# A hybrid layer's delta-rule scan: V and output of every other pair of heads in the other half of the partitions, and the streams' steps in a written order

## The chip, the cores and the metric

The kernel runs on one core of one Trainium2 chip. A core has five engines with queues of their own: TensorE for matmuls (PE; PEld is its weight load), VectorE (DVE), ScalarE (ACT), GpSimd (POOL) and SyncE (SP), which here issues most DMAs. The metric is the device time of one execution in microseconds; less is better.

## The reference

One decoder layer on 512 tokens of width 1024, all in float32. A normed input goes through one projection `w_in`; half of it feeds block-sparse attention with 8 heads, the other half a gated DeltaNet with 8 heads of width 64. Their outputs go side by side through `w_out`, then follow a residual, a norm and a squared-ReLU MLP of width 4096. The part that the change is about is the DeltaNet's scan over 8 chunks of 64 tokens:

```python
m = jnp.where(strict, jnp.einsum('bhnid,bhnjd->bhnij', k_beta, kc) * decay, 0.0)
a_mat = m + jnp.eye(C, dtype=jnp.float32)
rhs = jnp.concatenate([vc * bc[..., None], k_beta * jnp.exp(g_cum)[..., None]], axis=-1)
uw = lax.linalg.triangular_solve(a_mat, rhs, left_side=True, lower=True, unit_diagonal=True)
u, w = uw[..., :dh], uw[..., dh:]
attn_intra = jnp.einsum('bhnid,bhnjd->bhnij', qc, kc) * decay
...
def step(state, xs):
    u_c, w_c, q_c, k_c, a_c, gl = xs
    v_new = u_c - jnp.einsum('bhck,bhkv->bhcv', w_c, state)
    o = jnp.einsum('bhck,bhkv->bhcv', q_c, state) + jnp.einsum('bhcs,bhsv->bhcv', a_c, v_new)
    state = state * gl[..., None, None] + jnp.einsum('bhck,bhcv->bhkv', k_c, v_new)
    return state, o
```

## The kernel before

The large matmuls keep float32 accuracy by three products of a high and a low part (`mm3`: high by high, high by low, low by high); each operand is split by a cast on ACT (`w_hi`, `wo_h`, `mg_h`) and a subtraction on DVE or POOL (`w_lo`, `wo_l`, `mg_l`). The program has three stretches. From the start to about 250 us, PE makes the projections' matmuls (`ps_mm<-hT_h,w_hi` and the like), and attention, the chunks' matrices, their inverses and the scan are woven in between. The output projection (`output`, L953) follows up to about 294 us, and the MLP fills the rest.

What is woven are Python generators, called streams: `chunks` makes each pair's matrices (its `turned`, L533, copies gates into the tile `R` on ACT, PE transposes `R`, and ACT and DVE make `RC`, which PE multiplies by `picks`), `inverse` the triangular inverse, `scores` and `values` the attention, `scan` (L776) the delta rule, `finish_o` (L905) its norm, gate and transposes into `mg_h` and `mg_l`; `projections` (L279) is the filler. Each `yield` gives a stream's turn back. The class `Weave` (L49) keeps a modelled PE time, `now`, and always resumes the stream of the best `RANK` whose waiting time, given by the tables `WAIT` (L20) and `SINGLE` (L22), has passed. So PE's order is fixed by the program. On DVE, ACT and POOL a scheduler places the instructions, and a stream's `LEAD` says how far ahead of the others it may place them.

`scan` holds eight heads as four pairs. For chunk n of tokens (tile t, half c), a PSUM bank `B[n]` of 128 partitions gathers three products: the inverse times V (`ps_g<-vB,inv`, made one step ahead by `ahead`), the state `S` times `LWQ` (the operands for V and for the output side by side), and `AT` times V (`ps_g<-vn,AT`). V stands in partitions `cs` of the bank, the output in the other half `oc`; `rows_c` gives both. After `S`·`LWQ`, ACT copies V into `vn` (L870). Then PE makes the state's update (`ps_g<-vn,kdec`) and `AT`·V, with the next chunk's `inv`·`vB` in between:

```python
for h in range(8):
    if sp is not None:
        mm(sp[head(h), h // 2], kdec[cs, t, hs], V[cs, hs], start=True, stop=True)
        if h % 2:
            next(other)()
for h in range(8):
    mm(B[n][oc, h // 2, head(h)], AT[cs, h, t], V[cs, hs], start=n == h == 0, stop=True, skip_group_check=True)
    if h % 2 == 0:
        next(other, lambda: 0)()
```

An output at `head(h)` of the partitions alternates with h between the halves of PE's columns; one at `cs` or `oc` is in one half for the whole step. A small zero matmul (`z`, L855) opens the output's half of the bank. DVE then adds the update into the next state (L893), ACT copies the output to `ot` (L896).

`weights_out` (L935) loads and splits `w_out` in 16 pieces through two `wo_raw` buffers that the projections' loads use as well; SP issues them, ACT casts, DVE subtracts. `weights_up` (L1042) loads the first eight pieces of `w_up`, the last two (k=6, 7) through `w_raw`; `up0` (L1059) multiplies by them. In `normed` (L1010), SP writes a residual tile to `d_x`, and `output` loads the input tile `xs`. At the start, DVE zeroes rows of the two `RC` tiles (L530) ahead of `one`, which FILL=7 warm-up matmuls read in `head` (L217).

Of the kernel before, what the change touches and what calls it, by code (L numbers as in the profile page):

```python
# [35 lines left out]
class Delays(dict):  # L36


    def __init__(self, kinds, single):
        super().__init__(kinds)  # L40
        self.single = single
        self.count = {}

    def __getitem__(self, kind):
        n = self.count[kind] = self.count.get(kind, -1) + 1
        return self.single.get((kind, n), super().__getitem__(kind))


class Weave:  # L49

    def __init__(self, tc):
        self.tc = tc
        self.now = 0.0
        self.marks = {}
        self.live = []

    def spawn(self, rank, stream, lead=0):  # L60
        self.live.append([rank, self.now, stream, lead])
        self.live.sort(key=lambda s: s[0])

    def mark(self, name, wait=0.0):
        self.marks[name] = self.now + wait

    def start(self, s):
        return self.marks.get(s[1], math.inf) if isinstance(s[1], str) else s[1]

    def run(self, until=None):  # L70
        while self.live and not (until and until <= self.marks.keys()):
            s = next((s for s in self.live if self.start(s) <= self.now), None)
            if s is None:
                s = min(self.live, key=self.start)
                assert self.start(s) < math.inf, [s[1] for s in self.live]
                self.now = self.start(s)
            try:
                if s[3]:
                    with self.tc.high_priority(s[3]):
                        w = next(s[2])  # L80
                else:
                    w = next(s[2])
                s[1] = w if isinstance(w, str) else self.now + w
            except StopIteration:
                self.live.remove(s)


def layer(ctx, tc, nc, x, x_t, x_t0, w_first, w_in, w_v, w_ab, w_out, w_up, w_down, conv_w, a_log, dt_bias, gdn_norm_w, rel_bias,
# [9 lines left out]
    def mm(o, l, r, **kw):  # L98
        nc.tensor.matmul(o, l, r, **kw)  # L99
# [1456 lines left out]
```

## Time and profile before

| | |
|---|---|
| runs, median (lowest to highest) | 619.85 us (619.47 to 620.92), 3 runs |
| the profiled execution | 620.34 us; span 618.6 us |
| PE clock granted | 0.998 |
| PE busy 0 to 20 us | 20.00 |
| PE busy 20 to 165 us | 143.33 of 145 |
| PE busy 165 to 250 us (the scan) | 84.34 of 85 |
| PE busy 250 to 300 us | 50.00 |
| PE busy 300 to 618.6 us | 312.50 of 318.6 |

The time of a run is the span and 1.74 us around it. A busy PE need not be PE at its pace: records of matmuls overlap, and where they start further apart than usual, the record is longer, not the idle time. So time is to be read from starts, not from busy shares.

### The profile page before, as it was taken

Reading aid. Unit: us, or ns where it says so; the run is one execution under the profiler, and the core shown is the slowest. Engines: PE = TensorE matmul, PEld = TensorE weight load, DVE = VectorE, ACT = ScalarE, POOL = GpSimd, SP = SyncE. Lnnn points to the kernel's source line nnn. Section 1 sums busy time; section 2 is a strip of 40 time slices with the busy share of each in tenths; the row PEclk is TensorE's granted clock in tenths of the full one; section 3 lists DMA queues with packets and bytes.
Section 4 is the critical chain, followed back from the end, with each engine's and each line's share of the span. In section 5 each row is a group of like instructions: output and inputs, shape, how many; then the busy total and the mean of one; then the engine's idle time right before and its main releaser. Section 6 shows DMA issues by size and latency. Waiting matters only on the chain.

```text
span 618.6 us, 11048 instructions
## 1 busy us (share of the span) xinstructions
PE 607.9 (98%) x4295; PEld 521.9 (84%) x4295; DVE 474.4 (77%) x685; ACT 365.3 (59%) x625; POOL 139.1 (22%) x177
## 2 busy tenths in 40 slices
PE   8999999999999999999999999999999999999996
PEld 7777787878778877788999999999998888888884
DVE  7578873899734576766699878787788888888776
ACT  6479763453686376454338656656665656565663
POOL 0556746100322111025131121123111420000000
PEclk9999999999999999999999999999999999999999
DMA  9232334322721113933669999998999999967503
GB/s 317 84 109 72 95 79 102 105 84 85 173 81 58 52 36 103 315 128 117 242 217 255 225 267 310 263 239 220 237 322 311 304 293 286 310 217 288 183 0 137
DMA packets 61156, 113.22 MB, mean 183 GB/s; under 512 B 15784, under 2 KB 35368, under 8 KB 60720
## 3 DMA queue, kind: packets, MB, share of 16 engines
q1 hardware_dynamic: 43120, 82.89, 39.3%
q0 software_dynamic: 17696, 29.36, 22.8%
q8 instruction: 34, 0.56, 0.4%
q10 hardware_dynamic: 288, 0.26, 0.1%
q14 instruction: 18, 0.15, 0.1%
HBM read 106.71 MB, written 35.15 MB: 229 GB/s over the span
## 4 chain that ended last, share of the span: by engine, by line
PE 81%; issue 10%; DVE 3%; DMA 3%; ACT 2%; SPq 0%; POOLq 0%; DVEq 0%
PE ps_mm L99 40%; PE ps_g L99 22%; PE ps_a L99 16%; PE ps_a L103 2%; DMA wo_raw<-in_w_out 1%; DMA xy<-d_x 1%; PE ps_g L103 1%; DMA E<-d_e 1%; DVE wo_l L145 1%; ACT wo_h L144 0%; DVE L L694 0%; ACT L L696 0%; DVE conv L383 0%; DMA d_e<-L 0%; DVE S L893 0%
## 5 line engine op out<-in xcount | busy, mean ns | idle before, releaser
L132 ACT CAST wdh<-wd 128x1024 fp32r<-128x1024 f32 x53 | 55.9, 1054 | 51.3 <-PE ps_mm L99 22.6
L132 ACT CAST u_h<-w 128x1024 fp32r<-128x1024 f32 x49 | 50.9, 1045 | 52.5 <-DVE w L1166 15.6
L133 DVE TENSOR_TENSOR wdl<-wd,wdh 128x1024 fp32r<-128x1024 f32 x53 | 64.9, 1224 | 21.6 <-ACT wdh L132 21.5
L133 DVE TENSOR_TENSOR u_l<-w,u_h 128x1024 fp32r<-128x1024 f32 x49 | 59.9, 1224 | 23.9 <-ACT u_h L132 23.9
L99 PE MATMUL ps_mm<-hT_h,w_hi 128*128 128x512 f32 x168 | 70.2, 418 | 0.0
L99 PE MATMUL ps_mm<-hT_l,w_hi 128*128 128x512 f32 x168 | 66.0, 393 | 0.0
L99 PE MATMUL ps_mm<-hT_h,w_lo 128*128 128x512 f32 x168 | 65.8, 392 | 0.0
L1199 POOL DMA_DIRECT2D d_T<-in_w_down x32 | 33.0, 1043 | 145.6 <-DMA d_T<-in_w_down 90.7
L156 ACT CAST w_hi<-w_raw 128x512 fp32r<-128x512 f32 x50 | 31.0, 620 | 39.2 <-PE ps_g L99 15.4
L99 PE MATMUL ps_mm<-wdh,u_h 128*128 128x512 f32 x116 | 45.2, 390 | 0.0
L99 PE MATMUL ps_mm<-wdl,u_h 128*128 128x512 f32 x116 | 45.1, 389 | 0.0
L99 PE MATMUL ps_mm<-wdh,u_l 128*128 128x512 f32 x116 | 45.1, 389 | 0.0
L99 PEld LDWEIGHTS ps_mm<-hT_h,w_hi 128*128 128x128 f32 x168 | 31.7, 189 | 8.8 <-issue 2.6
L99 PEld LDWEIGHTS ps_mm<-hT_h,w_lo 128*128 128x128 f32 x168 | 31.5, 188 | 7.1
L99 PEld LDWEIGHTS ps_mm<-hT_l,w_hi 128*128 128x128 f32 x168 | 31.8, 189 | 5.2
L133 DVE TENSOR_TENSOR u_l<-f,u_h 128x1024 fp32r<-128x1024 f32 x28 | 34.1, 1218 | 0.0
L157 POOL TENSOR_TENSOR w_lo<-w_raw,w_hi 128x512 fp32r<-128x512 f32 x22 | 28.8, 1308 | 22.2 <-ACT w_hi L156 18.4
L99 PE MATMUL ps_g<-wdh,u_h 128*128 128x512 f32 x80 | 31.1, 389 | 0.0
L99 PE MATMUL ps_g<-wdl,u_h 128*128 128x512 f32 x80 | 31.1, 389 | 0.0
L99 PE MATMUL ps_g<-wdh,u_l 128*128 128x512 f32 x80 | 31.1, 389 | 0.0
L132 ACT CAST u_h<-f 128x1024 fp32r<-128x1024 f32 x28 | 29.3, 1046 | 0.0
L99 PEld LDWEIGHTS ps_mm<-wdh,u_h 128*128 128x128 f32 x116 | 21.8, 188 | 4.8 <-ACT c_u L1441 0.3
(486 smaller groups left out, 1841.4 us busy)
## 6 DMA issues: line engine op xcount, KB each, us to landing
d_T<-in_w_down POOLq DMA_DIRECT2D x48, 512.0 KB, 11.8
wd<-d_T SPq DMA_DIRECT2D x32, 512.0 KB, 6.3
w<-in_w_up SPq DMA_DIRECT2D x28, 512.0 KB, 8.1
wd<-in_w_down SPq DMA_DIRECT2D x24, 512.0 KB, 8.1
w_raw<-in_w_in SPq DMA_DIRECT2D x40, 256.0 KB, 2.6
wo_raw<-in_w_out SPq DMA_DIRECT2D x16, 256.0 KB, 3.5
d_T<-d_T POOLq DMA_DIRECT2D x8, 512.0 KB, 10.4
ww<-in_w_first SPq DMA_DIRECT2D x8, 256.0 KB, 5.4
```

Of the source, the lines that this page charges most:

```text
L99: nc.tensor.matmul(o, l, r, **kw)
L103: nc.tensor.transpose(o, i, ident[:k, :k])
L132: nc.scalar.copy(hi, src)
L133: tt(lo, src, f32(hi), op=OP.subtract)
L145: (sub or tt)(lo, raw, f32(hi), op=OP.subtract)
L156: nc.scalar.copy(hi, raw)
L157: (sub or tt)(lo, raw, f32(hi), op=OP.subtract)
L1199: nc.gpsimd.dma_start(d_T[t][k], block(b, second)[k], accum_op=OP.add, max_dma_last_dim=1024)
```

## The change

In `scan`, V and the output of pairs 1 and 3 (heads 2, 3, 6, 7) change places: `half(c ^ h // 2 % 2)` puts V of odd pairs in the other half of the partitions of `B[n]`. The order `TURNS` of the heads alternates between even and odd pairs, in `inv`·`vB` and in `AT`·V. The zero matmul is gone (the first two `inv`·`vB` of a bank open it). ACT copies V and the output in two instructions of half the width each; the tile `vn` holds V by parity of the pair. `w_of` and `q_of` swap the places of the two operands in `LWQ` for odd pairs; the negation into `LWQ` and, for q1 and q3, the last operation of `conv_silu` become two of half the size.

`Weave` loses its modelled time. A list `STEPS` names the streams in the order in which they are resumed; a name that isn't ready yet is passed over and stays in the list. The tables `WAIT`, `SINGLE`, `RANK` and `START` go. `LEAD` changes for six kinds, and `ORDER` swaps the projections v0 and v2. The two `RC` tiles are zeroed by POOL. Behind about 300 us the order is the same.

```diff
-RANK = {'chunks': 1, 'inverse': 4, 'scan': 2, 'scores': 4, 'values': 4, 'finish_o': 4, 'take': 3}
-LEAD = {'chunks': 300, 'inverse': 50, 'scan': 50, 'scores': 300, 'values': 50, 'finish_o': 200, 'take': 50, 'take_a': 300, 'scalars': 0}
+STEPS = "constants_in0 chunks1 constants_in0 bias0*3 chunks0 chunks2 chunks3 scalars0*2 ev0 ev1 ...
+LEAD = {'chunks': 100, 'inverse': 50, 'scan': 100, 'scores': 100, 'values': 300, 'finish_o': 200, 'take': 50, 'take_a': 100, 'scalars': 50}
+TURNS = 0, 2, 1, 3, 4, 6, 5, 7
...
-ORDER = "k0 q0 x0 y0 k1 q2 q1 k2 k3 z0 q3 x1 w0 v1 v3 v0 v2 y1 x2 y2 x3 y3 z2 z1 z3"
+ORDER = "k0 q0 x0 y0 k1 q2 q1 k2 k3 z0 q3 x1 w0 v1 v3 v2 v0 y1 x2 y2 x3 y3 z2 z1 z3"
...
-            s = next((s for s in self.live if self.start(s) <= self.now), None)
...
+            name = self.left.pop(next(i for i, name in enumerate(self.left) if self.ready(name)))
+            s = self.live[name]
...
         for t in RCs:
+            nc.gpsimd.memset(f32(t[32:64]), 0.0)
...
-    for t in RCs:
-        nc.vector.memset(f32(t[32:64]), 0.0)
...
-    w_of = lambda p: LWQ[p // 2][:, p % 2, :, 0:4:3]
-    q_of = lambda p: LWQ[p // 2][:, p % 2, :, 1:3]
+    w_of = lambda p: LWQ[p // 2][:, p % 2, :, 1:3] if p % 2 else LWQ[p // 2][:, p % 2, :, 0:4:3]
+    q_of = lambda p: LWQ[p // 2][:, p % 2, :, 0:4:3] if p % 2 else LWQ[p // 2][:, p % 2, :, 1:3]
...
-        stt(dst, f(th), 1.0, f(c), op0=OP.add, op1=OP.mult)
+        for n in ((slice(None), slice(None), 0), (slice(None), slice(None), 1)) if apart else (slice(None),):
+            stt(dst[n], f(th)[n], 1.0, f(c)[n], op0=OP.add, op1=OP.mult)
...
-            for h in range(8):
-                yield lambda h=h: mm(B[n][cs, h // 2, head(h)], UT[cs, h, t], vB[cs, t, 64 * h:64 * h + 64], start=h == 0, stop=False, skip_group_check=True)
-            if n:
-                z = SS[0][cs, 0, 64 - 64 * c:128 - 64 * c]
-                yield lambda: mm(B[n][oc, 0, :64], z, z, start=True, stop=False, skip_group_check=True)
+            for h in TURNS:
+                yield lambda h=h: mm(B[n][half(c ^ h // 2 % 2), h // 2, half(h % 2)], UT[half(c), h, t], vB[half(c), t, 64 * h:64 * h + 64], start=h in (0, 2), stop=False, skip_group_check=True)
...
-                V = sc.tile([128, 512], FT, name="vn", bufs=1)
+                V = sc.tile([128, 2, 2, 128], FT, name="vn", bufs=1)
+                v_of = lambda h: V[cs, h // 2 % 2, h // 4, half(h % 2)]
...
-            nc.scalar.copy(V[cs], B[n][cs].rearrange("p a b -> p (a b)"))
+            for s in range(2):
+                nc.scalar.copy(V[cs, s], of(B[n], s)[half(c ^ s)])
...
-            for h in range(8):
-                hs = slice(64 * h, 64 * h + 64)
-                mm(B[n][oc, h // 2, head(h)], AT[cs, h, t], V[cs, hs], start=n == h == 0, stop=True, skip_group_check=True)
-                if h % 2 == 0:
+            for i, h in enumerate(TURNS):
+                mm(B[n][half(1 - c ^ h // 2 % 2), h // 2, half(h % 2)], AT[cs, h, t], v_of(h), start=False, stop=True, skip_group_check=True)
+                if i % 2 == 1:
                     next(other, lambda: 0)()
...
-            nc.scalar.copy(o[cs], B[n][oc].rearrange("p a b -> p (a b)"))
+            for s in range(2):
+                nc.scalar.copy(of(wide(o), s)[cs], of(B[n], s)[half(1 - c ^ s)])
```

Three places show what the order makes of it. The first is the end of the scan's first step on PE (line, operation, output<-operands, size; line numbers differ between the two programs). Before, with `S` as the zero matmul and the projection's matmul behind it:

```order
L99 MATMUL ps_g<-vn,AT 64x64
L99 MATMUL ps_g<-vB,inv 64x64
L99 MATMUL ps_g<-vn,AT 64x64 x2
L99 MATMUL ps_g<-vB,inv 64x64
L99 MATMUL ps_g<-vn,AT 64x64 x2
L99 MATMUL ps_g<-vB,inv 64x64
L99 MATMUL ps_g<-vn,AT 64x64 x2
L99 MATMUL ps_g<-vB,inv 64x64
L99 MATMUL ps_g<-vn,AT 64x64
L99 MATMUL ps_g<-S_2333 64x64
L99 MATMUL ps_mm<-hT_h_83,w_hi 128x512
```

After:

```order
L82 MATMUL ps_g<-vn,AT 64x64 x2
L82 MATMUL ps_g<-vB,inv 64x64
L82 MATMUL ps_g<-vn,AT 64x64 x2
L82 MATMUL ps_g<-vB,inv 64x64
L82 MATMUL ps_g<-vn,AT 64x64 x2
L82 MATMUL ps_g<-vB,inv 64x64
L82 MATMUL ps_g<-vn,AT 64x64 x2
L82 MATMUL ps_g<-vB,inv 64x64
L82 MATMUL ps_mm<-hT_h_82,w_hi 128x512
```

The `AT` matmuls come by twos from different halves, and the zero matmul is gone. Ahead of this step's `kdec` part stood six matmuls of the projection, and there are fifteen now. For the chunks 1 to 7, the other streams' matmuls and transposes between `S`·`LWQ` and what follows of the scan number 8, 8, 3, 6, 11, 13, 6 before and 6, 11, 6, 6, 9, 16, 15 after; those between the step before and `S`·`LWQ` 6, 7, 24, 12, 3, 3, 6 and 6, 6, 15, 3, 20, 6, 9.

The second is PE between the last transposes of q's squares (`sqt`) and the second transposes of `R`. Before:

```order
L99 MATMUL ps_mm<-hT_h_82,w_lo 128x512
L99 MATMUL ps_mm<-hT_h_82,w_hi 128x512
L99 MATMUL ps_mm<-hT_l_84,w_hi 128x512
L99 MATMUL ps_mm<-hT_h_82,w_lo 128x512
L103 MATMUL ps_g<-ident,R 128x128 x4
L99 MATMUL ps_g<-RC_119,picks 128x512
L99 MATMUL ps_a<-RC_119,picks 128x256 x2
L99 MATMUL ps_g<-RC_119,picks 128x512
L99 MATMUL ps_mm<-hT_h_83,w_hi 128x512
```

After:

```order
L82 MATMUL ps_mm<-hT_h_83,w_lo 128x512
L82 MATMUL ps_mm<-hT_h_83,w_hi 128x512
L82 MATMUL ps_mm<-hT_l_85,w_hi 128x512
L82 MATMUL ps_mm<-hT_h_83,w_lo 128x512
L82 MATMUL ps_g<-RC_119,picks 128x512
L82 MATMUL ps_a<-RC_119,picks 128x256 x2
L82 MATMUL ps_g<-RC_119,picks 128x512
L85 MATMUL ps_g<-ident,R 128x128 x4
L82 MATMUL ps_mm<-hT_h_83,w_hi 128x512
```

The matmuls on `RC` now come ahead of the transposes of `R`; and between the first transposes of `R` (further up) and these stand 24 matmuls of a projection instead of 15.

The third is DVE ahead of the first `mg_l`, which the output projection reads. Before (`wo_l` is a piece of `w_out`, `om` and `zs` the gate of the scan's output, `ot` its norm):

```order
L145 TENSOR_TENSOR wo_l<-wo_raw,wo_h 128x512 x2
L453 SCALAR_TENSOR_TENSOR zs<-t_2899,zs 128x512
L914 TENSOR_TENSOR ot<-ot,oss 128x512
L145 TENSOR_TENSOR wo_l<-wo_raw,wo_h 128x512 x2
L450 SCALAR_TENSOR_TENSOR zs<-ps_mm,rstd_b 128x512
L453 SCALAR_TENSOR_TENSOR zs<-t_2951,zs 128x512
L923 SCALAR_TENSOR_TENSOR om<-ps_g,nw,zs 128x512
L145 TENSOR_TENSOR wo_l<-wo_raw,wo_h 128x512 x2
L133 TENSOR_TENSOR mg_l<-om,mg_h 128x4x128
```

After:

```order
L126 TENSOR_TENSOR wo_l<-wo_raw,wo_h 128x512 x2
L883 TENSOR_REDUCE oss<-osq 128x8
L126 TENSOR_TENSOR wo_l<-wo_raw,wo_h 128x512 x2
L433 SCALAR_TENSOR_TENSOR zs<-ps_mm,rstd_b 128x512
L887 TENSOR_TENSOR ot<-ot,oss 128x512
L436 SCALAR_TENSOR_TENSOR zs<-t_2958,zs 128x512
L896 SCALAR_TENSOR_TENSOR om<-ps_g,nw,zs 128x512
L126 TENSOR_TENSOR wo_l<-wo_raw,wo_h 128x512 x2
L114 TENSOR_TENSOR mg_l<-om,mg_h 128x4x128
```

Counted from the first `wo_l` of the program, eight stand ahead of `mg_l` before, nine after. On SP, the load of `w_raw` for k=6 of `w_up` moves behind the load of `xs` for tile 2, and that for k=7 behind the write of `d_x` of tile 2 and the load of `xs` for tile 3; both stood ahead of them.

More of the change, by code (lines that the diff above doesn't have):

```diff
@@ L29, with steps @@
 FIRST_BANKS = "mm g g a"
-START = (11.22, 9.92, 21.65, 14.65, 32.69, 16.13)
-ORDER = "k0 q0 x0 y0 k1 q2 q1 k2 k3 z0 q3 x1 w0 v1 v3 v0 v2 y1 x2 y2 x3 y3 z2 z1 z3"
+ORDER = "k0 q0 x0 y0 k1 q2 q1 k2 k3 z0 q3 x1 w0 v1 v3 v2 v0 y1 x2 y2 x3 y3 z2 z1 z3"
 LO_DVE = (22, 53)
 V_BANKS = "mm mm a g"
[L36 to L41, printed above, removed]
+def steps(text):
+    return [name for word in text.split() for name, _, n in [word.partition("*")] for _ in range(int(n or 1))]
@@ L42, in __init__, with spawn @@
+class Weave:
+    def __init__(self, tc, order):
+        self.tc = tc
+        self.left = list(order)
+        self.marks = set()
+        self.live = {}
         self.count = {}
-    def __getitem__(self, kind):
+    def spawn(self, stream, lead=0):
+        kind = stream.gi_code.co_name
         n = self.count[kind] = self.count.get(kind, -1) + 1
[L46 to L68, printed above, removed]
-    def run(self, until=None):
-        while self.live and not (until and until <= self.marks.keys()):
-            s = next((s for s in self.live if self.start(s) <= self.now), None)
[L73 to L76, printed above, removed]
-            try:
-                if s[3]:
-                    with self.tc.high_priority(s[3]):
-                        w = next(s[2])
-                else:
-                    w = next(s[2])
-                s[1] = w if isinstance(w, str) else self.now + w
@@ new lines, in spawn, with mark, ready @@
+        self.live[f"{kind}{n}"] = [None, stream, lead]
+    def mark(self, name):
+        self.marks.add(name)
+    def ready(self, name):
+        return name in self.live and (self.live[name][0] is None or self.live[name][0] in self.marks)
+    def run(self, until=None):
+        while self.live and not (until and until <= self.marks):
+            name = self.left.pop(next(i for i, name in enumerate(self.left) if self.ready(name)))
+            s = self.live[name]
+            try:
+                if s[2]:
+                    with self.tc.high_priority(s[2]):
+                        s[0] = next(s[1])
+                else:
+                    s[0] = next(s[1])
@@ L92, in layer @@
     act = nc.scalar.activation
-    weave = Weave(tc)
-    wait = Delays(WAIT, SINGLE)
+    weave = Weave(tc, steps(STEPS))
     mark, spawn = weave.mark, weave.spawn
@@ L696, in scores @@
                     act(l, l, AF.Exp, bias=mins[:, q, hh:hh + 1], scale=-1.0, accum_out=sums[:, q, hh:hh + 1])
-                yield wait["row"]
-                mark(f"row{p}{q}", wait["rows"])
+                yield
+                mark(f"row{p}{q}")
             nc.vector.reciprocal(sums, sums)
@@ L1095, in layer @@
     sc = pool("scan", 2, stack=sA, side="right")
[L1096 to L1100 removed]
+    spawn(scan(), LEAD["scan"])
+    spawn(weights_out())
+    spawn(output())
+    spawn(weights_up())
+    spawn(up0())
     weave.run()
```

177 lines of the change are left out of this document (81 added, 96 removed).

## The prediction

> **What bounds the kernel now.** I read the page first: the busy shares and the chain that ended last.
>
> ```profile
> PE 607.9 (98%) x4295; PEld 521.9 (84%) x4295; DVE 474.4 (77%) x685; ACT 365.3 (59%) x625; POOL 139.1 (22%) x177
> PE 81%; issue 10%; DVE 3%; DMA 3%; ACT 2%; SPq 0%; POOLq 0%; DVEq 0%
> ```
>
> PE is busy 607.9 of 618.6 us, and the chain names PE for 81%. So PE's own time counts, and with it the 10.7 us in which PE idles; other engines matter where PE waits for them. The next view groups instructions of one form from 165 to 250 us, where the scan runs (busy and mean count overlapping records, so they only rank).
>
> ```profile
> L99 PE MATMUL ps_g<-vB,inv 64*64 64x64 f32 x128 | 11.0, 228 | 0.0
> L99 PE MATMUL ps_g<-vn,AT 64*64 64x64 f32 x128 | 8.8, 218 | 0.0
> L99 PE MATMUL ps_g<-vn,kdec 64*64 64x64 f32 x112 | 4.8, 224 | 0.0
> L870 ACT COPY vn<-ps_g 64x512 f32<-64x512 f32 x8 | 4.6, 578 | 3.7 <-PE ps_g L99 3.6
> ```
>
> Among the scan's small matmuls, those on `inv`·`vB` and `vn`·`AT` cost 11.0 and 8.8 us of busy time against 4.8 for `vn`·`kdec`, although their counts (128, 128, 112) are alike. The timeline of one scan step (start, length, engine, operation) shows why; each f32 matmul leaves two records.
>
> ```profile
> 210.22 0.27 PE L99 MATMUL ps_g<-vn,kdec 64*64 64x64 f32 x2
> ...
> 210.73 0.22 PE L99 MATMUL ps_g<-vn,AT 64*64 64x64 f32 x1
> ...
> 211.75 0.50 PE L99 MATMUL ps_mm<-hT_h,w_hi 128*128 128x512 f32 x1
> ```
>
> From 210.22 to 210.73, 0.51 us, eight `kdec` matmuls run, four of the next chunk's `inv`·`vB` among them. The `AT` part holds eight and four again, and two records of a zero matmul, yet takes from 210.73 to 211.75, 1.02 us. In the code, the `kdec` results alternate between the two column halves of PE, while all eight `AT` results of a step go to one. The ends of the scan show the same, as one window's rows ahead of the other's:
>
> ```profile
> 187.83 1.09 PE L99 MATMUL ps_g<-vB,inv 64*64 64x64 f32 x16
> 188.85 0.50 PE L99 MATMUL ps_mm<-hT_h,w_hi 128*128 128x512 f32 x1
> ...
> 232.25 1.14 PE L99 MATMUL ps_g<-vn,AT 64*64 64x64 f32 x16
> 233.32 0.50 PE L99 MATMUL ps_mm<-hT_h,w_hi 128*128 128x512 f32 x1
> 233.66 0.39 PE L99 MATMUL ps_mm<-hT_l,w_hi 128*128 128x512 f32 x1
> 233.89 0.39 PE L99 MATMUL ps_mm<-hT_h,w_lo 128*128 128x512 f32 x1
> ```
>
> The first eight `inv`·`vB` take 1.02 us and the last eight `AT` 1.07 us, alone on one quarter of the array: 16 records at 0.064. The projection's matmuls behind them start every 0.23.
>
> The waits of PE's weight loads (total, times, longest) are the second thing to read:
>
> ```profile
> PEld ps_a L99 <- DVE rs L207: 2.2, 1, 2.2
> PEld ps_g L99 <- ACT vn L870: 1.4, 4, 0.5
> PEld ps_g L99 <- DVE S L893: 1.1, 2, 0.8
> PEld ps_mm L99 <- DVE mg_l L133: 0.6, 1, 0.6
> ```
>
> The four sum to 5.3 us; `rs` is the program's start, `vn` and `S` the scan, `mg_l` the entry into the output projection.
>
> **Alternating halves in the scan.** With `TURNS`, an `AT` phase has the make-up of a `kdec` phase: eight matmuls by turns in two column halves, four others beside them. I give it 0.51 us from that phase, and the zero matmul goes. Seven steps save 1.02 − 0.51 = 0.51 each, 3.6. Eight matmuls by turns alone I also put at 0.51: the first `inv`·`vB` saves 0.5, the last `AT` 0.55. Sum 4.6. Bounds: 0, if the halves don't overlap here; 5.2, if the phases run at 0.064 × 8 = 0.51 less the last record's tail of some 0.07.
>
> The Trainium skill, "TensorE: Matmul & The Clock Gate", section "Wait — 56ns, not 53.3ns?", says that with hardware decode off each MATMUL takes the sequencer some 62 ns. An estimate by that page is 12 × 62 = 0.74 for a phase of twelve, and the scan term 3.0. The trace disagrees: twelve take 0.51 above, so the measurement decides.
>
> The price is on ACT: the copy of V (0.578 above) and that of the output become two of half the width.
>
> ```profile
> L722 ACT COPY ph<-ps_a x24: 372/530/592, 128.8 to 244.9; 128x512 f32<-128x512 f32 x12, 128x384 f32<-128x384 f32 x8, 128x256 f32<-128x256 f32 x4
> ```
>
> The nearest narrow copy, 128x256, is this group's minimum, 0.372. Two end 0.74 − 0.58 = 0.17 later than one, the first 0.2 earlier. Sixteen pairs are 2.7 us of ACT at most, which is 59% busy; only V's second half is waited for, and part of the matmuls there need just the first half. The LWQ negations, likewise halved, and the q convolution's last operation, halved on DVE, are issued tens of us ahead of use; PE's waits name neither convolution nor q. All of these I cost at nothing: if the cover were gone, some 0.17 a step, 1.4.
>
> **Waits in the scan.** `vn` and `S` cost 1.4 + 1.1 = 2.5 us. The written order mostly puts longer fillers there: ahead of the first `kdec` phase, six matmuls of a projection become fifteen, ahead of the fourth three (0.69 at 0.23 each) become six; ahead of `S`·`LWQ`, the three at the fifth and sixth chunks become twenty mixed ones and six. S needs, behind `kdec`, two additions:
>
> ```profile
> L893 DVE TENSOR_TENSOR S<-S,ps_g x2: 414/419/424, 210.9 to 211.4; 64x256 f32<-64x256 f32 x2
> ```
>
> In the step from 210.22 they end by 211.85, 1.6 after its start. The new step lasts 1.02, so a filler of 0.6 covers it where DVE is free; two places keep about that (three matmuls of a projection; six short ones on `pt`), and there a busy DVE could cost what it does now, up to 0.8, and half a us more for the shorter step. `V` has one short place left (six on `pt`; now the longest wait there is 0.5). I leave 0.4 for `V` and 0.9 for `S`, 1.3 of 2.5, and gain 1.2. Bounds: −0.5 (two times 0.8 + 0.5 for `S`, 0.4 for `V`) and 2.3 (almost all).
>
> **The start.** DVE zeroes two RC tiles before `one`, which the warm-up matmuls read.
>
> ```profile
> 0.76 0.52 POOL L1086 MEMSET R<- 128x512 f32 x1
> 0.89 1.03 DVE L531 MEMSET RC<- 32x512 f32 x2 [0.89 <-PEq L1548]
> 2.24 3.35 PE L99 MATMUL ps_a<-one 128*128 128x128 f32 x14 [2.24 <-DVE rs L207]
> 4.09 0.43 DVE L261 CAST w_hi<-ww 128x512 fp32r<-128x512 f32 x1 [1.83 <-DMA ww<-in_w_first]
> 7.53 1.02 PE L99 MATMUL ps_g<-hT_l,w_hi 128*128 128x512 f32 x2
> 8.38 0.40 PE L99 MATMUL ps_a<-hT_l,w_hi 128*128 128x512 f32 x1
> 8.62 0.40 PE L99 MATMUL ps_mm<-hT_h,w_lo 128*128 128x512 f32 x1
> ```
>
> Without the 1.03 us on DVE, `one` comes 1.03 earlier, and the warm-up runs from 1.2 to about 4.55. The first real operand (`w_hi`, 4.09 + 0.43 = 4.52) is there just then. So the first real matmul moves up about 0.85 (warm-up ends near 5.4 now). PE runs at half pace, 0.425, until 8.38, and at 0.23 behind. If the change of pace stays at 8.38, two more matmuls are done by then, worth 0.4; if it moves with the first matmul, the gain is 0.85 to 1.0. I take 0.7; bounds 0.3 and 2.1 (rival 3). POOL's two fills cost about 0.52 each by R's row; nothing of POOL's is waited for by PE in that stretch, and RC is first read near 60 us. If that cover failed, 1.0.
>
> **Order ahead of the scan.** The transposes of `R` for pair 1 wait for ACT's copies into `R`, which follow on the transposes for pair 0.
>
> ```profile
> 53.27 0.60 PE L103 MATMUL ps_g<-ident,R 128*128 128x128 f32 x4
> ...
> 59.98 0.66 PE L103 MATMUL ps_g<-ident,R 128*128 128x128 f32 x4 [1.08 <-ACT R L536]
> 60.61 0.46 PE L99 MATMUL ps_g<-RC,picks 128*128 128x512 f32 x1
> ```
>
> PE idles 1.08 before 59.98. Between the two sets stand 15 matmuls of a projection now; in the new order 24 do, and the `RC`·`picks` matmuls come ahead of the second set. From the first set's end at 53.87, PE would be there after 24 × 0.23 = 5.5, the two sets of `sqt` transposes like those of R, 1.2, and three `picks`, 0.7: 7.4, by 61.3 in this trace's time, so that the wait ending at 59.98 is gone. Late next is RC, wanted 6.7 behind the first set, at 60.6; it was there by 60.61, so nothing much is left. Gain 1.0 here, of 1.08. From 90 to 160 us others change places with projections too, which I take as 0 in sum. Other moves can open new waits, of which this trace can't show any; the nearest row is this one. Bounds −1, one such wait beside the gain given up, and 1.1, this wait gone.
>
> **Entry into the output projection.** SP's `wo_raw` loads go through two buffers, and ACT waits for their landings; `mg_l` stands behind the `wo_l` on DVE.
>
> ```profile
> 242.42 0.63 ACT L144 CAST wo_h<-wo_raw 128x512 fp32r<-128x512 f32 x1 [1.48 <-DMA wo_raw<-in_w_out]
> 245.41 0.62 ACT L144 CAST wo_h<-wo_raw 128x512 fp32r<-128x512 f32 x1
> 246.41 0.63 ACT L144 CAST wo_h<-wo_raw 128x512 fp32r<-128x512 f32 x1
> ...
> 246.54 1.28 DVE L145 TENSOR_TENSOR wo_l<-wo_raw,wo_h 128x512 fp32r<-128x512 f32 x2
> 247.74 0.68 DVE L133 TENSOR_TENSOR mg_l<-om,mg_h 128x512 fp32r<-128x512 f32 x1
> ```
>
> ```profile
> w_raw<-in_w_in SPq DMA_DIRECT2D x40, 256.0 KB, 2.6
> wo_raw<-in_w_out SPq DMA_DIRECT2D x16, 256.0 KB, 3.5
> ```
>
> PE reaches the third output matmul 0.3 before `mg_l` is done (the 0.6 above, at the loads). Now nine `wo_l` instead of eight stand ahead of `mg_l`: one more cast costs 1.0 if it is the second of a pair (245.41 to 246.41) and 3.0 if it must wait for a landing (242.42 to 245.41). Against that, PE comes earlier by the part of the gain that lies behind the point where the loads begin, about 3.4 us of scan, which frees buffers earlier as well (the same projections' weights hold them). I take a loss of 1.0; bounds 0.5 gain and 3.0 loss. All of `output` is queued behind it on PE, so nothing hides it.
>
> **The last `w_up` loads.** SP issues `w_raw` of k=6 and 7 at 266.55 now; in the new order k=7 stands behind the write of tile 2's `d_x` and the load of `xs` for tile 3.
>
> ```profile
> 291.28 0.33 SPq L973 DMA_DIRECT2D xs<-in_x  x1
> ...
> 293.58 0.28 PE L99 MATMUL ps_mm<-ma_h,wu 128*128 128x256 f32 x1
> ```
>
> It would issue at 291.61 in this trace's time, land 2.6 later (the row of `w_raw`), and pass one cast (0.62) and one subtraction (0.69): 295.5. PE begins `wu` at 293.58 and needs k=7 after 21 matmuls of 0.12, 296.1. Slack 0.6; with a landing of 3.5, like `wo_raw`, a loss of 0.3. I take 0.3; bounds 0 and 1.5. Behind 300 us the order is the same on all engines and shifts as a whole: 0.
>
> **Sum.** 4.6 + 1.2 + 0.7 + 1.0 − 1.0 − 0.3 = 6.2. The profiled execution took 620.34, span 618.6 and 1.74 around it: 614.1. The median of the runs, 619.85, stands 0.49 lower, so I forecast 613.7.
>
> **Rivals.**
> 1. The halves don't overlap for `AT`, because the stationary operand's rows or the shared bank matter. For it: the first `inv`·`vB` runs at one quarter's pace. Against: `kdec` at 0.51 is the same case. The scan term falls to 0.1 (the zero matmuls hardly count: the last step, without one, takes 1.07): 618.2. Chance 0.06.
> 2. The `wo_raw` loads don't come earlier at all, and the ninth waits for a landing. Then PE meets `mg_l` 3.4 + 3.0 = 6.4 late instead of 1.0: 613.7 + 5.4 = 619.1, no change. Slower follows if a further landing (3.5) comes on top: 622.6; the deciding point is 8.4 us of waiting at the first `mg_l`. For it: ACT idles 1.48 for a landing already. Against: the two buffers are released by projections that come earlier with PE. Chance 0.11, half of it slower.
> 3. The pace of PE opens early. It opened at 8.38, with PE busy from 2.24, so perhaps a whole stretch of fixed length must be busy; with the warm-up at 1.2 an earlier stretch is full. The seven matmuls between 5.4 and 8.38 would then run at 0.23: 7 × 0.2 = 1.4 more, 612.3. Chance 0.2. The Trainium skill, same page, section "What's actually happening", gives a free-running window of about 3.4 us that has to be busy; by it the estimate is an opening at 8.38 − 3.41 = 4.97. No row here shows the window.
> 4. The new order opens a wait ahead of the scan that costs 3 or more: 616.7 and up. For it: most waits in the list are of that stretch. Against: PE's fillers there are plenty. Chance 0.1.
>
> **How the numbers follow.** The sum as it stands has 0.53, rival 3 0.2: both faster. Rivals 1 and 4 end faster by over 0.2% (1.24 us, about what a measurement of this kernel can tell from no change) but for some 0.02. Rival 2 splits. Faster 0.87, same 0.07, slower 0.06. The range: adding the bounds of two large terms at a time gives about ±3; rival 3 and a full `S` gain reach 610.8 below, rival 4 617 above; what is left out is rivals 1 and 2, 0.17, and the far part of rival 4.
>
> **What would show it.** In the trace after: an `AT` phase of 0.5 instead of 1.02; no `ps_g<-S` 64x64 rows; `vn` and `S` together at 1.3 or less in the waits; warm-up from 1.2 and the change of pace at 7.3 to 8.4, or 5.0 by rival 3; a wait for `mg_l` of 1 to 2; the `wu` matmuls without a gap at k=7. The prediction is wrong if `AT` stays at 1.0, if `mg_l` waits 6 or more, or if new waits of over 3 us stand between 20 and 165 us.

## The result

The kernel after the change takes 616.56 us in the median of five runs (616.02 to 617.53), the one before 619.87 (619.47 to 620.92): a ratio of 0.9947 with a 95% interval of 0.9932 to 0.9961. It is faster by 3.3 us. The forecast was 613.7, a gain of 6.2; the sign held, and nearly half of the gain didn't come. The profiled execution after took 617.12, with a span of 615.3 and a granted clock of 0.997.

The page of the kernel after, busy times and the chain that ended last: PE is still busy for 98%, and the chain's share on DMA went from 3 to 5%.

```profile
PE 604.2 (98%) x4281; PEld 516.7 (84%) x4281; DVE 475.5 (77%) x685; ACT 369.0 (60%) x645; POOL 138.0 (22%) x179
PE 78%; issue 9%; DMA 5%; DVE 4%; ACT 1%; POOL 1%; SPq 0%; POOLq 0%; ACTq 0%; DVEq 0%
```

The same groups as the prediction showed, from 165 to 250 us (count | busy, mean ns | idle before). The `AT` group went from 8.8 to 5.1 us of busy time and now stands beside `kdec`; ACT copies V 16 times at 368 ns instead of 8 times at 578.

```profile
L82 PE MATMUL ps_g<-vB,inv 64*64 64x64 f32 x128 | 8.3, 239 | 0.0
L82 PE MATMUL ps_g<-vn,AT 64*64 64x64 f32 x128 | 5.1, 219 | 0.0
L82 PE MATMUL ps_g<-vn,kdec 64*64 64x64 f32 x112 | 4.9, 225 | 0.0
L847 ACT COPY vn<-ps_g 64x256 f32<-64x256 f32 x16 | 5.9, 368 | 3.4 <-PE ps_g L82 3.1
```

The timeline of one scan step and of the scan's two ends in the kernel after:

```profile
185.79 0.64 PE L82 MATMUL ps_g<-vB,inv 64*64 64x64 f32 x16
186.36 0.50 PE L82 MATMUL ps_mm<-hT_h,w_hi 128*128 128x512 f32 x1
...
207.19 0.27 PE L82 MATMUL ps_g<-vn,kdec 64*64 64x64 f32 x2
...
207.71 0.22 PE L82 MATMUL ps_g<-vn,AT 64*64 64x64 f32 x1
...
208.27 0.50 PE L82 MATMUL ps_mm<-hT_h,w_hi 128*128 128x512 f32 x1
...
231.28 0.68 PE L82 MATMUL ps_g<-vn,AT 64*64 64x64 f32 x16
231.89 0.50 PE L82 MATMUL ps_mm<-hT_h,w_hi 128*128 128x512 f32 x1
```

The `AT` part runs from 207.71 to 208.27, 0.56 us where it took 1.02; the first eight `inv`·`vB` take 0.57 (186.36 − 185.79) where they took 1.02, the last eight `AT` 0.61 where they took 1.07. The whole step went from 1.53 to 1.08.

The waits of PE's weight loads after (total, times, longest). `vn` and `S` fell from 1.4 and 1.1 to 0.7 and 0.2. At the top of the list is a new one, for `ph`.

```profile
PEld ps_a L82 <- ACT ph L700: 1.6, 1, 1.6
...
PEld ps_g L82 <- ACT vn L847: 0.7, 2, 0.4
...
PEld ps_mm L82 <- ACT mg_h L113: 0.6, 1, 0.6
...
PEld ps_mm L82 <- DVE mg_l L114: 0.5, 1, 0.5
...
PEld ps_g L82 <- DVE S L865: 0.2, 1, 0.2
```

Since busy records overlap, I compare the starts of the same PE matmuls in the two traces. Each row is the time from one landmark's start to the next one's:

| stretch of PE | before | after | difference |
|---|---|---|---|
| start to first `ps_g<-L,abw` | 30.11 | 29.15 | −0.96 |
| to first `inv`·`vB` (the scan's start) | 157.72 | 156.64 | −1.08 |
| to the last matmul of `AT`·V | 45.34 | 45.96 | +0.62 |
| to the first matmul of the output projection | 14.44 | 11.34 | −3.10 |
| to first `wu` | 45.97 | 45.83 | −0.14 |
| to the last `ps_g<-mg_l,w_hi` of that tile | 24.51 | 25.54 | +1.03 |
| to the last matmul of the MLP | 294.02 | 293.81 | −0.21 |
| to the end of the span | 6.49 | 7.03 | +0.54 |

The third and fourth rows belong together: the new order moved other streams' work out of the fourth into the third, and three projection matmuls (0.69) from the second. Taken so, the stretch ahead of the scan gained 0.39 of its own and the scan with the entry into the output projection 3.17.

### The profile page after: what moved, and what is told of

It is laid out like the page before. It is cut to its first block, busy times and chain, and to the rows that moved or that the text cites. A ratio compares the mean times of both kernels' runs of the same rounds, so it can differ in the third digit from the quotient of the medians.

```text
span 615.3 us, 11043 instructions
## 1 busy us (share of the span) xinstructions
PE 604.2 (98%) x4281; PEld 516.7 (84%) x4281; DVE 475.5 (77%) x685; ACT 369.0 (60%) x645; POOL 138.0 (22%) x179
## 4 chain that ended last, share of the span: by engine, by line
PE 78%; issue 9%; DMA 5%; DVE 4%; ACT 1%; POOL 1%; SPq 0%; POOLq 0%; ACTq 0%; DVEq 0%
PE ps_mm L82 40%; PE ps_g L82 20%; PE ps_a L82 16%; DMA wo_raw<-in_w_out 2%; PE ps_a L85 2%; DMA xy<-d_x 1%; PE ps_g L85 1%; DMA w_raw<-in_w_up 1%; DVE wo_l L126 1%; POOL rkq L175 1%; DVE xs L995 0%; DMA ww<-in_w_first 0%; DMA w_raw<-in_w_in 0%; DVE conv L365 0%; ACT wo_h L125 0%
## 5 line engine op out<-in xcount | busy, mean ns | idle before, releaser
L138 DVE TENSOR_TENSOR w_lo<-w_raw,w_hi 128x512 fp32r<-128x512 f32 x28 | 22.1, 790 | 5.0 <-ACT w_hi L137 4.9
```

Of the source, the lines that this page charges most:

```text
L138: (sub or tt)(lo, raw, f32(hi), op=OP.subtract)
```

## The experiments

Each was timed in five rounds beside the kernel before, whose median was 619.82 to 620.08 in the three sittings. My theory by the traces: the layout saves what it should in the scan, and the missing part is lost at three places behind it or beside it, at the entry into the output projection (ACT's queue behind landings), at the last `w_up` loads, and in waits that were never worth what they were listed at. The rivals: the written order alone makes the gain, or the layout's gain depends on the order. The first four runs tell these apart.

**The new layout in the old order** (before, with `TURNS`, `half(c ^ h // 2 % 2)` and the halved copies, and `Weave` with its modelled time kept):

```diff
+TURNS = 0, 2, 1, 3, 4, 6, 5, 7
...
-            for h in range(8):
-                yield lambda h=h: mm(B[n][cs, h // 2, head(h)], ...
+            for h in TURNS:
+                yield lambda h=h: mm(B[n][half(c ^ h // 2 % 2), h // 2, half(h % 2)], ...
```

> The kernel before, with the scan's new layout alone (other half of the partitions for pairs 1 and 3, alternating order of the heads, no zero matmul, halved copies); the planner's tables and PE's order around it stay. Theory A (the alternation is worth what its phases save, and the old order can turn it into time): each AT part falls from 1.02 us to about 0.57, as in the changed kernel, eight times, and the first inv-vB likewise: 4.1 us less PE time; S then waits up to 0.5 longer at the two places with three matmuls only, so 3 to 4 us faster, 616 to 617 us. Rival B (the written order is what makes room for it): in the old order the freed time turns into waits for S and vn, which rise from 2.5 us to over 4, and the kernel gains less than 2 us, 618 or more.

Measured: 620.23, ratio 1.0012 (1.0002 to 1.0021): no gain at all. Yet the matmuls overlap as in the kernel after (first `inv`·`vB` 0.57, last `AT` 0.61). Its waits say where the 4.1 us went:

```profile
PEld ps_g L100 <- ACT vn L873: 2.8, 5, 1.5
...
PEld ps_g L100 <- DVE S L892: 2.0, 2, 1.2
```

Before, these two were 1.4 and 1.1. From the scan's start to its last `AT` it gained 1.9 us, not 4.1. It lost 0.8 ahead of the scan, where PE now idles 0.96 for `RC`, and 0.8 in the output projection, where PE idles 0.34 for DVE's step on `xs`. (The 0.9 that its profile gained ahead of the first `ps_g<-L,abw` comes from an earlier change of pace; see the last section.) PE's order is that of the kernel before, the zero matmul and the turns aside, so shorter steps mostly uncover the waits for V and for the state when the fillers stay where they were.

**The written order with the old layout** (after, with the scan's layout of before):

```diff
-            for h in TURNS:
-                yield lambda h=h: mm(B[n][half(c ^ h // 2 % 2), h // 2, half(h % 2)], ...
+            for h in range(8):
+                yield lambda h=h: mm(B[n][cs, h // 2, head(h)], ...
```

> The changed kernel with the scan's old layout (eight AT and eight inv-vB results of a step in one column half, the zero matmul, full copies); the written order, leads and POOL's zeroing stay. Theory A (the two parts add up): start 0.96, waits ahead of the scan 0.4, waits inside the scan 0.75, less 1.65 at the output projection's entry, 1.03 at the last w_up loads and 0.5 at the end leave about -1 to +1: 619 to 621 us, no change. Rival B (the order is the larger part, by shorter waits): 2 us or more faster, 617.9 or less. Rival C (the entry's wait exists only because the scan is faster): the entry costs nothing here, 618 to 619.

Measured: 622.25, 1.0038 (1.0026 to 1.005), slower. The loss is at the last `w_up` load, where the stretch from `wu` takes 28.42 instead of 24.51. The wait there, and SP's and ACT's rows of the load:

```profile
PEld ps_mm L82 <- ACT w_hi L137: 2.0, 1, 2.0
```

```profile
289.41 0.76 SPq L132 DMA_DIRECT2D w_raw<-in_w_up  x1
...
295.15 0.62 ACT L137 CAST w_hi<-w_raw 128x512 fp32r<-128x512 f32 x1 [2.91 <-DMA w_raw<-in_w_up]
```

The load is issued at 289.41 and lands by 295.15, 5.7 us later. PE idles 1.79 for it, and right behind that the granted clock is 0.50 for 3.42 us (the column behind POOL's; the ones ahead are the stretch, its length and the busy time of PE, PEld, DVE, ACT and POOL):

```profile
296.06:299.48 3.42, 3.31 (x15) 3.00 (x15) 3.39 (x5) 1.19 (x3) 0.00 (x0) 0.50 0.00 0
```

Half the clock for 3.42 us is worth some 1.7 us by estimate, so the wait and the clock behind it make most of the 3.9.

**The last `w_up` loads earlier** (`up_early`: after, with two steps of the list moved):

```diff
-... output0*6 normed0 normed1 output0*6 weights_up0 output0*9 normed2 output0 normed0 output0 weights_up0 output0 normed1 ...
+... output0*6 weights_up0*2 normed0 normed1 output0*15 normed2 output0 normed0 output0*2 normed1 ...
```

> The changed kernel with the steps that load k=6 and 7 of w_up moved ahead of the first normed step, so that SP issues them ahead of d_x and xs as before. Theory A (the 1.03 us that PE loses around k=7 come from that load's late issue, 4.2 us ahead of its landing): no wait for w_hi and w_lo there, 1.0 us faster than the changed kernel, about 615.5. Rival B (the loads that they are moved ahead of are then late, or PE waits there for something else next, such as the transposes of tile 3): less than 0.3 us, 616.3 to 616.8.

Measured: 615.34, 0.9927 (0.9915 to 0.9939), the fastest of all kernels here. The stretch from `wu` is back at 24.51, and the median is 1.2 lower than the kernel after's.

**Four pieces of `w_out` split on POOL** instead of ACT and DVE (after):

```diff
+POOLED = 5, 6, 7, 8
...
+                    if len(W) in POOLED:
+                        nc.sync.dma_start(raw, src)
+                        nc.gpsimd.tensor_copy(wh[:, k], raw)
+                        nc.gpsimd.tensor_tensor(wl[:, k], raw, f32(wh[:, k]), op=OP.subtract)
```

> The changed kernel with the cast and the subtraction of w_out's pieces 5 to 8 on POOL instead of ACT and DVE. Theory A (at the output projection's entry PE waits for ph, 1.5 us, and mg_h, 0.5 us, because these stand behind casts on ACT that wait for wo_raw to land): the ph copies start when PE has made their input, the two waits go, and the kernel is 1.5 to 2 us faster than the changed one, about 614.8. Rival B (the landing of the pieces is what PE needs anyway): PE waits as long at the first output matmuls for wo_h or wo_l, less than 0.3 us gained. Rival C (POOL's norm of the scan's output, oss, now stands behind the casts): om and so mg_h come later, PE waits longer, slower than the changed kernel by 1 us or more.

Measured: 621.18, 1.0017 (1.0007 to 1.0027). It took the wait from ACT's queue and put a longer one into POOL's: `oss`, a small step of `finish_o`, now stands behind the casts, and PE's transposes of `ot` wait for it:

```profile
245.38 0.63 PE L86 MATMUL ps_g<-ident,ot 128*128 128x128 f32 x4 [4.09 <-DVE ot L888]
```

Behind that wait the granted clock is 0.50 from 246.23 to 249.64, so the run pays twice. It tells nothing on what ACT's wait costs; the run without the loads, below, does.

The rest, but for one that is named, were made on top of the early `w_up` loads, so that this loss is out of the way.

**The old layout again, with the written order and early `w_up`** (the layout's edit of above, on `up_early`):

> The scan's old layout in the written order, with the loads of k=6 and 7 of w_up early. Theory A (the old layout lost 3.9 us at the late w_up loads for a reason that is not the layout's): that loss goes, 618.4 us; against the changed kernel with the early loads (615.3) the layout is then worth 3.1 us in the written order, where it was worth nothing in the old one. Rival B (the loss sat elsewhere): 621 to 622, and the layout would seem worth 6.

Measured: 618.28, 0.9976 (0.9967 to 0.9985). That makes a table of two by two, in medians:

| | old layout | new layout |
|---|---|---|
| old order | 619.85 | 620.23 |
| written order, early `w_up` | 618.28 | 615.34 |

The layout is worth 2.9 us in the written order and nothing in the old one; the written order alone (with its leads and POOL's zeroing) 1.6, about half of it from the start (below). So my theory holds for the written order only, and the rival that the layout's gain hangs on the order is right. By starts, it saves 4.1 from the first `inv`·`vB` to the last `AT` (50.08 to 45.99) and gives back 1.2 from there to the output projection (9.92 to 11.14). That this makes 2.9 again is partly chance: the two profiled spans differ by 1.8 only, since `up_early` also took 0.45 longer ahead of the scan and 0.6 longer at the end.

**Pairs one after the other** (on `up_early`):

```diff
-TURNS = 0, 2, 1, 3, 4, 6, 5, 7
+TURNS = 0, 1, 4, 5, 2, 3, 6, 7
```

> The changed kernel with early w_up loads and TURNS = 0, 1, 4, 5, 2, 3, 6, 7: the four heads of the even pairs first, then the four of the odd pairs, so that the same results fall into the same halves of the columns, but not by turns. Theory A (what counts is that neighbours in the queue sit in different column halves): an AT part takes about 1.0 us again, as does the first inv-vB, +3 to 4 us of PE time; with the longer waits given back, 617.5 to 619 against 615.3. Rival B (it is enough that the work is spread over both halves, in any order): 0.57 a part, 615.3, no change.

Measured: 617.09, 0.9957 (0.9944 to 0.997), 1.75 slower than `up_early`. Here four matmuls in a row go to one half of the columns. The timeline of a step: the `AT` part takes 0.85 (190.27 to 191.12), between 0.56 by turns and 1.02 in one half.

```profile
190.27 0.22 PE L82 MATMUL ps_g<-vn,AT 64*64 64x64 f32 x1
...
191.12 0.50 PE L82 MATMUL ps_mm<-hT_h,w_hi 128*128 128x512 f32 x1
```

**The zeroing back on DVE** (on `up_early`), and **the zeroing alone moved to POOL** (on the kernel before):

```diff
-            nc.gpsimd.memset(f32(t[32:64]), 0.0)
...
+    for t in RCs:
+        nc.vector.memset(f32(t[32:64]), 0.0)
```

> The changed kernel with early w_up loads, with the two RC tiles zeroed by DVE at the start, as before. Theory A (the zeroing holds back the warm-up matmuls, and with them the first projection and on average the change of PE's pace): warm-up from 2.24 instead of 1.08, 0.5 to 1.0 us slower, 615.9 to 616.3. Rival B (the change of pace comes at a time of its own, whatever the warm-up does): 0.2 us at most, 615.3 to 615.5.

> The kernel before, with the RC tiles zeroed by POOL instead of DVE and nothing else. Theory A (the start is worth the same in both programs): warm-up from 1.08, first projection's matmul about 0.5 earlier; on average 0.7 to 1.5 us faster than before, 618.4 to 619.1. Rival B (the gain is lost in the old order's waits, as the scan's was): within 0.4 of before, 619.4 to 619.9.

Measured: 616.83, 0.9948 (0.9935 to 0.9961), 1.5 slower than with POOL; and 619.19, 0.9989 (0.9979 to 0.9999), 0.9 faster than the kernel before. By starts of `ps_g<-L,abw` the two are worth 0.67 and 0.97. Single profiles scatter there by more than that (last section). In the eleven kernels with POOL's zeroing this start lies between 28.17 and 29.30, 28.65 in the mean; in the three with DVE's between 28.84 and 30.11, 29.40 in the mean. So the zeroing is worth about 0.75 by starts; why the medians of the first pair differ by 1.5 stays open.

**`w_out` not loaded** (on `up_early`; an identity is cast in its place, so `w_out` is left out of the result):

```diff
+UNLOADED = range(16)
...
+                        nc.scalar.copy(f4(wh[:, k]), ident[:, None, :].to_broadcast([128, 4, 128]))
```

> The changed kernel with early w_up loads; the 16 pieces of w_out aren't loaded, the casts and subtractions read the identity matrix instead (so w_out is left out of the result, and ACT's and DVE's instructions for it stay). Theory A (at the output projection's entry PE waits 1.1 us for ph and 0.9 for mg_h because both stand behind casts that wait for loads): both waits go, out of PE's time from the last scan step to the output's first matmul, about 1.7 us faster, 613.6. Rival B (ph and mg_h wait for their own inputs: the scores' sums, the norm of the scan's output): less than 0.5 us, 614.8 to 615.4. Rival C (the casts, runnable at once, crowd ACT and DVE where the scan needs them): slower than 615.3.

Measured: 616.07, 0.994 (0.9927 to 0.9952), 0.7 slower than `up_early`. At the place in question the expected happened: from the last `AT` to the output projection PE took 9.12 us instead of 11.14, and waits for `ph`, `mg_h` and `mg_l` are gone. But without landings to hold them back, the casts and subtractions run early and crowd ACT and DVE inside the scan. Its waits:

```profile
PEld ps_g L83 <- ACT vn L848: 2.4, 3, 1.7
PEld ps_g L83 <- DVE S L866: 1.3, 2, 1.2
```

That stretch took 48.37 instead of 45.99 and ate the gain. So without the loads the entry is 2.0 us shorter; their lateness also keeps ACT free for the scan.

**The old `LEAD`** (on `up_early`):

```diff
-LEAD = {'chunks': 100, 'inverse': 50, 'scan': 100, ...
+LEAD = {'chunks': 300, 'inverse': 50, 'scan': 50, ...
```

> The changed kernel with early w_up loads and the old table LEAD (chunks and scores 300, scan and values 50, take_a 300, scalars 0): PE's order stays, the scheduler places DVE's and ACT's work by the old leads. Theory A (the longer fillers on PE are what covers S and V): waits for vn and S stay below 1.3 us together, time within 1 us of 615.3. Rival B (it was the scan's higher lead that let DVE and ACT answer in time): vn and S wait 2.5 us or more as before, 617 or more.

Measured: 616.33, 0.9941 (0.993 to 0.9953), 1.0 slower than `up_early`. `vn` waits 0.7 and `S` 0.2, as with the new leads, so it is the fillers of the written order that cover the scan's waits, and not the leads. Entry waits are a little longer (`mg_h` 1.1).

**Two of the last `values` steps (the transposes) earlier in the list**, so that `ph` is copied before the casts that wait (on `up_early`), called `entry_order`, and on top of it, `entry_buffer`, **with pieces 2 and 5 of `w_out` in a third buffer**:

```diff
-... projections0*3 scan0 finish_o3 weights_out0 projections0*2 ev15 finish_o3 ev15 projections0 values0 weights_out0 values0 ...
+... projections0 values0 projections0*2 scan0 finish_o3 weights_out0 values0 projections0*2 ev15 finish_o3 ev15 projections0 weights_out0 ...
```

```diff
+THIRD = (2, 5)
...
+                               raw=sc.tile([128, 512], FT, name="wo_raw", tag="kB", bufs=1) if len(W) in THIRD else wpool.tile(...
```

> The changed kernel with early w_up loads, and the transposes of the last scores (L, R) moved ahead of the last nine and six matmuls of the projection, so that ACT finds ph's input earlier and its two copies stand ahead of the waiting casts of w_out. Theory A (ph's place behind a waiting cast costs 1.1 us): no wait for ph, and the output's first matmul about 1 us earlier against the last AT; 614.3. Rival B (mg_h and mg_l stand behind the ninth piece anyway, whose load has not moved): the wait for ph turns into one for mg_h or mg_l, less than 0.4 us gained, 615.0 to 615.4.

> As entry_order, and pieces 2 and 5 of w_out are loaded into a third buffer (that of kB, free by then), so that later pieces are asked for earlier. Theory A (what holds the entry is the pace of the loads through two buffers): ACT's waits for wo_raw shrink, mg_h and mg_l come earlier, 1.5 us or more faster than 615.3, 613.8 or less. Rival B (the scheduler fills the room with more casts ahead of mg_h, twelve instead of nine): no earlier mg_l, 615 to 616. Rival C (SP's loads in order wait for the new buffer): slower.

Measured: 617.48, 0.9961 (0.9948 to 0.9974), and 622.62, 1.0041 (1.0025 to 1.0057); both slower than `up_early`. The wait for `ph` went, and others took its place. The waits of the first and of the second:

```profile
PEld ps_g L85 <- DVE om L896: 1.5, 1, 1.5
...
PEld ps_mm L82 <- DVE mg_l L114: 1.1, 1, 1.1
```

```profile
PEld ps_g L86 <- DVE om L897: 3.6, 1, 3.6
PEld ps_mm L83 <- ACT mg_h L114: 3.0, 1, 3.0
```

Whatever stands behind the `wo_raw` landings on ACT or DVE waits; another order only picks which. In `entry_order` the entry itself is no longer than in `up_early` (10.94 against 11.14); the loss, 2.2, lies between the first output matmul and `wu`, where PE idles 0.67 for `mg_l` and the granted clock is 0.50 from 243.82 to 247.23. In `entry_buffer` the ninth load is issued 2.2 earlier, so the buffers did hold it back, but thirteen casts of `wo_h` instead of nine now stand ahead of `mg_h`, and PE idles 3.39 and 2.78 for `om` and `mg_h`; the granted clock is 0.50 from 244.88 to 251.71.

## Why the prediction was right in sign and 2.9 us off

| term | predicted | in the traces |
|---|---|---|
| phases of the scan | 4.6 | 4.1 |
| waits in the scan | 1.2 | 0.65 |
| start (single profiles) | 0.7 | 0.96 |
| order ahead of the scan | 1.0 | 0.4 |
| entry into the output projection | −1.0 | −1.6 |
| last `w_up` loads | −0.3 | −1.0 |
| elsewhere, the end among it | 0 | −0.2 |
| sum | 6.2 | 3.3 |

**Phases.** The mechanism was right. The size was 0.5 too large, since I gave an `AT` phase the 0.51 of `kdec`; after, it takes 0.56, and the ends 0.57 and 0.61. Seven steps save 0.45 each, the ends 0.45 and 0.46: 4.1. The run with the old layout in the same order gives 4.1 too. ACT's half copies took 368 ns against the 372 assumed, hidden. Twelve matmuls in 0.56 stand once more against the 0.74 estimated by the Trainium skill, "TensorE: Matmul & The Clock Gate", section "Wait — 56ns, not 53.3ns?", whose 62 ns for each holds with hardware decode off. The trace doesn't show 62 ns for each, and no run here shows which decode was on.

**Waits in the scan.** They fell by 1.6 at the weight loads, and I took such a fall for PE's time. But a weight load's wait isn't PE's: part of it passes while earlier matmuls still run. In the trace before, PE's own rows show just two short gaps for `S`, 0.34 and 0.15, and after none:

```profile
219.34 1.16 PE L99 MATMUL ps_g<-S,LWQ 128*128 128x128 f32 x8 [0.34 <-DVE S L893]
...
229.67 1.16 PE L99 MATMUL ps_g<-S,LWQ 128*128 128x128 f32 x8 [0.15 <-DVE S L893]
```

The two gaps sum to 0.49. The 0.65 of the table is a remainder: with the 4.1 of the phases and the −1.6 of the entry it makes the 3.17 of scan and entry.

**The start.** The warm-up starts at 1.08, as forecast, but then PE waits for its first operand:

```profile
1.08 3.36 PE L82 MATMUL ps_a<-one 128*128 128x128 f32 x14 [1.08 <-DVE rs L188]
4.74 0.77 PE L82 MATMUL ps_mm<-hT_h,w_hi 128*128 128x512 f32 x1 [0.30 <-DVE w_hi L241]
...
6.99 0.63 PE L82 MATMUL ps_g<-hT_l,w_hi 128*128 128x512 f32 x2
7.47 0.39 PE L82 MATMUL ps_a<-hT_l,w_hi 128*128 128x512 f32 x1
```

PE waits 0.30 for `w_hi`, so the first matmul moves up by 0.51 instead of 0.85. The pace changes near 7.0 instead of 8.38, a little ahead of the 7.3 to 8.4 that I gave, and brings another 0.45. POOL's two fills (0.98 us from 1.35) hold nothing up. Where the pace changes in a single profile is luck (last section); over all kernels the start is worth about 0.75, close to the 0.7.

**The order ahead of the scan.** At the place named, it went as worked out: `RC`·`picks` at 59.71, the second transposes of `R` at 60.42, no wait between, and the stretch around them 1.01 shorter (55.33 to 54.32). The step that failed is "the others change places, which I take as 0 in sum": two later stretches, up to the scan's start, lost 0.27 and 0.34.

**The entry.** I named `mg_l` behind nine `wo_l`. It waits 0.5, but the first and longest wait is for `ph`. ACT's rows, then PE's (start, length, [idle before <- releaser]):

```profile
236.29 0.62 ACT L125 CAST wo_h<-wo_raw 128x512 fp32r<-128x512 f32 x1 [0.97 <-DMA wo_raw<-in_w_out]
237.84 0.62 ACT L125 CAST wo_h<-wo_raw 128x512 fp32r<-128x512 f32 x1 [0.93 <-DMA wo_raw<-in_w_out]
238.48 1.07 ACT L700 COPY ph<-ps_a 128x512 f32<-128x512 f32 x2
...
239.12 2.37 PE L82 MATMUL ps_a<-ph,V 128*64 128x128 f32 x16 [1.34 <-ACT ph L700]
...
243.09 0.50 PE L82 MATMUL ps_mm<-wo_h,mg_h 128*128 128x512 f32 x1 [0.34 <-ACT mg_h L113]
243.42 0.40 PE L82 MATMUL ps_mm<-wo_l,mg_h 128*128 128x512 f32 x1
243.90 0.50 PE L82 MATMUL ps_mm<-wo_h,mg_l 128*128 128x512 f32 x1
```

Two casts of `wo_h` stand ahead of the `ph` copy in ACT's queue and idle 0.97 and 0.93 for landings; `ph` is copied at 238.48, PE idles 1.34. With 0.34 at `mg_h` and some 0.25 at `mg_l` PE loses 1.9, against 0.3 before. The chain that ended last, followed back from there, is the two buffers taking turns (start, length, what):

```profile
234.64 3.17 DMA wo_raw<-in_w_out
...
237.84 0.63 ACT wo_h L125
...
238.49 0.70 DVE wo_l L126
...
239.21 2.67 DMA wo_raw<-in_w_out
```

Each load can start only when the subtraction of the piece before last is done, so the pieces have a pace of their own: 4.6 us for one buffer's turn (234.64 to 239.21), 22.7 from the first load of `w_out` to the ninth (216.48 to 239.21). The first load does move with PE, from 221.65 before to 216.48, but what PE gains behind it isn't followed in full: from `order_up` to `up_early` the last `AT` comes 3.7 us earlier, the ninth load 2.8 (241.01 to 238.20). That is the account that the prediction gave for its −1.0; what it missed is ACT's queue, where `ph` stands behind the waiting casts. Rival 2 took it that the loads don't come earlier at all, which the trace contradicts; its ninth piece does wait for a landing (ACT idles 0.46 ahead of that cast), and the loss is a quarter of its price.

**The `w_up` loads.** The queueing behind `d_x` and `xs` was right; the landing was 4.2 us, not the 2.6 of `w_raw` in general or the 3.5 that I used as the bad case (the same two loads took 3.3 and 3.5 in the trace before). SP's, ACT's and PE's rows:

```profile
286.07 0.33 SPq L996 DMA_DIRECT2D d_x<-xs  x1
286.57 0.33 SPq L946 DMA_DIRECT2D xs<-in_x  x1
286.95 0.75 SPq L132 DMA_DIRECT2D w_raw<-in_w_up  x1
...
291.19 0.62 ACT L137 CAST w_hi<-w_raw 128x512 fp32r<-128x512 f32 x1 [1.39 <-DMA w_raw<-in_w_up]
...
291.86 0.39 PE L82 MATMUL ps_mm<-mg_h,w_hi 128*128 128x256 f32 x1 [0.28 <-ACT w_hi L137]
...
292.59 0.39 PE L82 MATMUL ps_mm<-mg_h,w_lo 128*128 128x256 f32 x1 [0.22 <-DVE w_lo L138]
```

With 4.2 my own working gives 297.1 against 296.1, a loss of 1.0: the measured one. The old layout in the same order had the same issue 2.0 us ahead of `wu` and a landing of 5.7, and lost 3.9, some 1.7 of them by the halved clock behind the wait. Moving the two steps took the loss away.

**The end.** From the start of the last matmul to the end of the span it is 6.5 us in the four traces with the old layout and in `wo_pool`, and 7.0 to 7.1 in the other nine with the new one. The instructions are the same up to ACT's last store, which is issued 3.3 us behind that matmul in the former and 3.6 (4.2 in `entry_buffer`) in the latter. So these 0.5 us seem to go with the program; why stays open.

**The rivals.** 1 (no overlap of halves) fell with the step of 1.08. 2 fell as it was put: the loads do come earlier and none of the waits is 6 us; that they have a pace of their own was right. 3 (the pace opens early): the change of pace came 5.9 us after the first warm-up matmul, in the trace before 6.1, so the kernel after didn't show it; see the last section. 4 (a wait of 3 us ahead of the scan) is in none of the traces.

## What to carry to other kernels

Splitting results between column halves of the array pays where the small matmuls alternate one by one; its worth then depends on what is there to fill the latencies that it uncovers, so layout and order are to be costed together (nothing and 2.9 us here). A gain that PE makes while a chain of loads through few buffers is under way is given back as far as that chain has its own pace: follow one buffer's turn, landing, cast and subtraction, and look at what else stands in the queue of the engine that waits for landings. Where a load is moved behind others on one queue, take its landing from a row with the same neighbours, not from the median of its kind. And where a run loses more than PE's idle time, read the granted clock behind the wait.
